# Order of ScalarE's copies at the first FFN pair, and the last FFN chunk in two passes over the token columns

## The chip, the core and the metric

The kernel runs on one core of a Trainium2 chip. The core has a matrix engine (TensorE, PE in the profile, its weight loads listed as PEld), VectorE (DVE), ScalarE (ACT), GpSimd (POOL) and SyncE (SP), which issues most of the DMAs. Each engine works through its own queue in order and waits for the others by semaphores. Matrix products are summed in PSUM; all else lies in SBUF. The metric is the device time of one execution in microseconds (us); lower is better.

## What is computed

One step of a one-layer hybrid encoder on 512 prompt tokens, 16 meta tokens and 32 sample tokens: RMSNorm, one input projection, a gated linear attention branch and a softmax branch, their gated sum, an output projection, then the feed-forward part and a last RMSNorm:

```python
m = jax.nn.sigmoid(ga) * ya + jax.nn.sigmoid(gb) * yb
h = h + jnp.einsum('btd,de->bte', m, w_out)
u = jnp.einsum('btd,df->btf', _rmsnorm(h, norm_ffn), w_up)
h = h + jnp.einsum('btf,fd->btd', jnp.square(jax.nn.relu(u)), w_down)
...
y_prompt = _rmsnorm(h_p[:, N_META:], norm_final)
y_sample = _rmsnorm(h_s, norm_final)
```

The model width is 1024 (8 blocks of 128), the FFN width 4096. All is float32.

## The kernel before

Activations lie transposed: 128 features on the partitions, the tokens along the free dimension. From the output projection on there are 544 token columns (32 of the sample, 512 of the prompt). To be exact in the fast float32 mode of the matrix engine, each operand is split into a rounded part (`split_hi`, a copy on ScalarE, line 121) and a rest (`split_lo`, a subtraction on VectorE, line 124), and each product is three matmuls: hi by hi, lo weight by hi, hi weight by lo. All matmuls have one helper and so one line (118); tiles tell them apart.

**Order.** From the output projection on, TensorE, ScalarE and VectorE run in exactly the order in which the program emits their instructions. SP's DMAs wait for the buffer that they write.

**Output projection (`ps_wo`).** Eight steps n over the output blocks d in the order 0, 4, 1, 5, 2, 6, 3, 7. A step splits the weights of the next block (`wh`, `wl`), runs 48 matmuls, adds the result to the residual (line 1237) and calls `operands(d)`. That function makes the FFN's right-hand operands: for d < 4 one pair of half-width tiles; for d of 4 or more, sums and differences (lines 1214 to 1221) and the splits called BN, B21 and BT4 (tiles `hh`, `hl`). Steps 1, 3, 5 and 7 have d of 4 or more.

**FFN, upward (`up_pair(g)`, 16 pairs).** Each pair makes four column groups of u by a seven-product scheme on halves (272 tokens wide): products of 12 matmuls into two PSUM tiles X and V that are copied out and then added to further, and Y. In order: X from a11, V from s1, X from s2, V from s4, X from s3, Y from a12, X from a22. X's product from s2 may start only when `fa` has taken the first X out of PSUM (ScalarE, line 1335); V's product from s4 only when `fb` has taken V (line 1341). Then comes relu squared (lines 1362, 1369) and its splits (`uh`, `ul`); those of the second half are put into the list `tail` and emitted in the next pair, ahead of `fa`'s copy. The weights of pair g+1 are prepared meanwhile by the generator `pair_prep` in seven steps: four DMAs (tile `wr`, three buffers), the sums s31 and s24 on VectorE (lines 287, 290, 294), the splits of a11, s1, then s2 and s4 together, then s3 and a12, then a22. Before pair 0 all of that is emitted ahead of the first copy of X.

**FFN, downward (`down(c, d)`).** Eight chunks c of 512 rows, eight output blocks d; 24 matmuls each, 288 and 256 columns wide in two PSUM tiles. Chunk c runs between the products of the pairs of chunk c+1; its weights come from `down_prep` (a DMA into `dr`, then the splits `dh`, `dl`, two buffers each). The first chunk's first weights are split in pair 2, just ahead of `down(0, 0)`. Results are summed into `acc`; the last chunk's are scaled by `r2`, added to the residual (lines 1423, 1425), and finished.

**The end.** The last chunk has no pairs beside it. `final_part(g, tiles)` transposes a group of blocks back to token rows (groups of 4, 3 and 1 blocks; line 1280, tile `ps_fin`), sums squares on ScalarE (line 1282) and multiplies by the weight on VectorE (line 1283, `ytok`). Tile 0 is the sample (32 tokens), tiles 1 to 4 are 128 prompt tokens each. `final_norm` makes the reciprocal root (lines 1296 to 1298, 399 to 401), scales (600 columns on VectorE, line 1305, 424 on ScalarE, line 1306) and starts the output DMAs (line 1308). Group 0 runs inside d = 4, group 1 inside d = 7, group 2 after it: tiles 0 to 2 after the first 288 columns, tiles 3 and 4 after the other 256.

Of the kernel before, what the change touches and what calls it, by code (L numbers as in the profile page):

```python
# [8 lines left out]
F32 = mybir.dt.float32  # L9
# [38 lines left out]
def tile_hybrid_step(  # L48
# [256 lines left out]
    def down_prep(c, d):  # L305

        if c == NCH - 1:
            raw = wpool.tile([P, K4, P], F32, tag="raw", name=f"dr{c}_{d}", bufs=3)
        else:
            raw = blk([K4, P], F32, f"dr{c}_{d}", "v")  # L310
        SP.dma_start(raw, w_down[0, 512 * c: 512 * c + 512, P * d: P * d + P].rearrange("(k p) n -> p k n", p=P))
        yield
        hi, lo = [pairw["L"].tile([P, K4, P], F32R, tag="d" + x, name=f"d{x}{c}_{d}", bufs=2) for x in "hl"]
        split_hi(hi, raw)
        split_lo(lo, raw, hi)
        downs[c, d] = (hi, lo)
        yield
# [875 lines left out]
    def operands(d, mid=None):  # L1193
        j, g = d % 4, gffn[:, d: d + 1]
        H_, L_ = hH[j], hL[j]

        def hi(i, src):
            split_hi(H_[:, i: i + src.shape[1], :], src)

        def lo(i, src):  # L1200
            split_lo(L_[:, i: i + src.shape[1], :], src, H_[:, i: i + src.shape[1], :])


        if d < 4:
            ba, bb = bts[0] = half_pair(f"ba{j}"), half_pair(f"bb{j}")
            ACT.activation(ba[:, 0, :], hs[d][:, 0:HT], AF.Copy, scale=g)
            ACT.activation(bb[:, 1, :], hs[d][:, HT:], AF.Copy, scale=g)
            DVE.tensor_tensor(ba[:, 1, :], ba[:, 0, :], bb[:, 1, :], ALU.subtract)
            hi(B11, ba)
            lo(B11, ba)  # L1210
            return
        ba, bb = bts[0]
        b2 = half_pair(f"b2{j}")
        ACT.activation(b2, halves(hs[d]), AF.Copy, scale=g)
        DVE.scalar_tensor_tensor(bb[:, 0, :], ba[:, 1, :], -1.0, b2[:, 1, :], ALU.mult, ALU.subtract)
        DVE.tensor_tensor(bb[:, 1, :], b2[:, 1, :], bb[:, 1, :], ALU.subtract)
        if mid:
            mid()
        hi(BN, bb)
        hi(B21, b2)  # L1220
        DVE.scalar_tensor_tensor(ba[:, 0, :], bb[:, 0, :], -1.0, b2[:, 0, :], ALU.mult, ALU.subtract)
        lo(BN, bb)
        hi(BT4, ba[:, 0:1, :])
        lo(B21, b2)
        lo(BT4, ba[:, 0:1, :])

    bts = [None]
    for n, d in enumerate(WO_ORDER):
# [12 lines left out]
        hs[d] = xr
        operands(d, (lambda: go(prep, 1)) if n == KD - 1 else None)
# [41 lines left out]

    s3b = cpool.tile([P, NTT], F32, name="s3b")

    def final_early():

        DVE.tensor_tensor(s3b, s3[:, :, 0], s3[:, :, 1], ALU.add)
        DVE.tensor_scalar(s3b, s3b, 1.0 / D, EPS, ALU.mult, ALU.add)  # L1290

    def final_norm(t0, t1):
        w = t1 - t0
# [22 lines left out]
                mm(ps[:, :HT], w[w_][:, j, :], x_[j][:, b, :], start and n == 0, n == 11)  # L1316
                n += 1

    tail = []

    def up_pair(g):

        nonlocal prep
        drain(prep) if g == 0 else None
        W = pairs.pop(g)
        uh = upool.tile([P, 4, HT], F32R, tag="uh", name=f"uh{g}")
        ul = upool.tile([P, 4, HT], F32R, tag="ul", name=f"ul{g}")
        us[g] = (uh, ul)
        fa, fb = half_pair(f"fa{g}"), half_pair(f"fb{g}")
        X, V = psm(f"ps_x{g}"), psm(f"ps_v{g}")  # L1330
        xv, vv = X[:, :HT], V[:, :HT]
        product(X, W["a11"], B11, True)
        while tail:
            tail.pop(0)()
        ACT.activation(fa[:, 0, :], xv, AF.Copy)  # L1335
        go(prep, 1)
        prep = pair_prep(g + 1) if g < 15 else iter(())
        go(prep, 1)
        yield
        product(V, W["s1"], BM, True)  # L1340
        ACT.activation(fb[:, 1, :], vv, AF.Copy)
        yield
        product(X, W["s2"], BN, False)
        ACT.activation(fa[:, 1, :], xv, AF.Copy)
        go(prep, 1)
        yield
        product(V, W["s4"], B22, False)
        go(prep, 1)
        DVE.tensor_tensor(fa[:, 1, :], vv, fa[:, 1, :], ALU.add)
        yield  # L1350
        product(X, W["s3"], BT3, False)
        x3 = fpool.tile([P, HT], F32, tag="x3", name=f"x3_{g}", bufs=1)
        go(prep, 1)
        ACT.activation(x3, xv, AF.Copy)
        DVE.tensor_tensor(fb[:, 1, :], x3, fb[:, 1, :], ALU.add)
        yield
        Y = psm(f"ps_y{g}")
        yv = Y[:, :HT]
        product(Y, W["a12"], B21, True)
        go(prep, 1)  # L1360
        DVE.tensor_tensor(fa[:, 0, :], yv, fa[:, 0, :], ALU.add)
        DVE.scalar_tensor_tensor(fa, fa, 0.0, fa, ALU.max, ALU.mult)
        yield
        product(X, W["a22"], BT4, False)
        split_hi(uh[:, 0:2, :], fa)
        go(prep, 1)
        split_lo(ul[:, 0:2, :], fa, uh[:, 0:2, :])
        ACT.activation(fb[:, 0, :], xv, AF.Copy)
        DVE.scalar_tensor_tensor(fb, fb, 0.0, fb, ALU.min, ALU.mult)

        def rest():
            split_hi(uh[:, 2:4, :], fb)
            split_lo(ul[:, 2:4, :], fb, uh[:, 2:4, :])

        tail.append(rest)
        yield
# [8 lines left out]
            dpreps[i] = down_prep(*dn[i])  # L1385
            go(dpreps[i], 1)

    def down(i, mid=None):
        c, d = dn[i]
        if i + 1 < len(dn):  # L1390
            go(dpreps[i + 1], 1)
        dstart(i + 2)
        wh, wl = downs.pop((c, d))
        psf = (psa, pss)[d % 2]
        pd = [psf(f"ps_dn{c}_{d}_{ci}") for ci in range(2)]
        for ci, ks in (((0, (0, 1)), (1, (0, 1)), (0, (2, 3)), (1, (2, 3))) if d == 0 else
                       ((0, range(4)), (1, range(4)))):
            a, b = OC[ci]
            if mid and ci == 1:
                mid()  # L1400
            for k in ks:
                uh, ul = [u[:, 2 * (k % 2): 2 * (k % 2) + 2, :].rearrange("p s t -> p (s t)")
                          for u in us[2 * c + k // 2]]
                for m, (w_, x_) in enumerate(((wh, uh), (wl, uh), (wh, ul))):
                    mm(pd[ci][:, : b - a], w_[:, k, :], x_[:, a:b], k == 0 and m == 0, k == 3 and m == 2)
        for ci in range(2):
            evac_down(c, d, ci, pd[ci])

    def evac_down(c, d, ci, ps):
        a, b = OC[ci]  # L1410
        w = b - a
        if c == 0:
            if ci == 0:
                acc[d] = blk([TM], F32, f"acc{d}", "v")
            ACT.activation(acc[d][:, a:b], ps[:, :w], AF.Copy)
        elif c < NCH - 1:
            DVE.tensor_tensor(acc[d][:, a:b], ps[:, :w], acc[d][:, a:b], ALU.add)  # L1417
            if c == NCH - 2:
                DVE.tensor_tensor(acc[d][:, a:b], acc[d][:, a:b], r2[:, a:b], ALU.mult)
                DVE.tensor_tensor(hs[d][:, a:b], acc[d][:, a:b], hs[d][:, a:b], ALU.add)  # L1420
        else:
            dt_ = fpool.tile([P, TM], F32, tag="dt", name=f"dt{c}_{d}_{ci}", bufs=2)
            DVE.tensor_tensor(dt_[:, :w], ps[:, :w], r2[:, a:b], ALU.mult)
            if d < 7 or ci == 0:
                DVE.tensor_tensor(hs[d][:, a:b], hs[d][:, a:b], dt_[:, :w], ALU.add)
            if d == 7:
                tiles = ((0, 1, 2), (3, 4))[ci]
                final_part(2, tiles, (dt_, a) if ci else None)
                final_norm(tiles[0], tiles[-1] + 1)

    def square(d):

        if d == 0:
# [17 lines left out]
    for c in range(NCH):  # L1451
        for jj in range(2):
            slots = up_pair(2 * c + jj)
            for n, _ in enumerate(slots):
                if c > 0 and n in (1, 3, 5, 6):
                    d = 4 * jj + (1, 3, 5, 6).index(n)
                    if d == 0 and c == 1:
                        go(dpreps[0], 1)
                    down(8 * (c - 1) + d)
                    if c == 1:  # L1460
                        square(d)
# [44 lines left out]
```

## Time and profile before

| | us |
|---|---|
| median of three runs | 850.74 (850.53 to 851.29) |
| profiled execution | 847.04 |
| span of its profile (first to last instruction) | 845.2 |

The profiled execution has 1.84 us around its span and lies 3.70 us under the median of the runs. In the page's first part TensorE is busy 96% of the span, VectorE 69%, ScalarE 43%. In the second part (40 slices of 21.1 us) TensorE's digit is 9 in nearly all slices; it falls to 7 and 6 in the slices that begin at 444 and 465 us and to 3 in the last one, from 824 us. A row of a timeline has the start, the time, engine, line, operation, output and inputs, shape and count, and in brackets the idle time before it with what ended it. A merged row of several instructions gives the time from the first start to the last end; matmuls overlap, so the pitch of a row of n is its time less that of one, over n - 1.

### The profile page before, as it was taken

Reading aid. Unit: us, or ns where it says so; the run is one execution under the profiler, and the core shown is the slowest. Engines: PE = TensorE matmul, PEld = TensorE weight load, DVE = VectorE, ACT = ScalarE, POOL = GpSimd, SP = SyncE. Lnnn points to the kernel's source line nnn. Section 1 sums busy time; section 2 is a strip of 40 time slices with the busy share of each in tenths; the row PEclk is TensorE's granted clock in tenths of the full one; section 3 lists DMA queues with packets and bytes.
Section 4 is the critical chain, followed back from the end, with each engine's and each line's share of the span. In section 5 each row is a group of like instructions: output and inputs, shape, how many; then the busy total and the mean of one; then the engine's idle time right before and its main releaser. Section 6 shows DMA issues by size and latency. Waiting matters only on the chain.

```text
span 845.2 us, 15168 instructions
## 1 busy us (share of the span) xinstructions
PE 808.9 (96%) x6087; PEld 776.3 (92%) x6087; DVE 583.7 (69%) x1139; ACT 367.1 (43%) x723; POOL 122.9 (15%) x131
## 2 busy tenths in 40 slices
PE   8999999999999999999997699999999999999993
PEld 7877889898999999999997699999999999999993
DVE  6865348798758564466677856787777777779884
ACT  6760454555445633232445465433433443344233
POOL 4315111121122393025000000000000000000000
PEclk9997999999999999999999999999999999999997
DMA  8612214421521133233321322333333333322112
GB/s 243 165 51 82 50 43 103 122 77 50 134 77 50 51 85 91 85 91 111 97 82 50 106 69 77 88 88 101 100 100 101 88 100 101 91 80 81 50 50 106
DMA packets 133813, 75.38 MB, mean 89 GB/s; under 512 B 15056, under 2 KB 129024, under 8 KB 133744
## 3 DMA queue, kind: packets, MB, share of 16 engines
q1 hardware_dynamic: 132704, 72.27, 30.4%
q0 software_dynamic: 1024, 2.14, 1.1%
q8 instruction: 48, 0.79, 0.4%
q14 instruction: 21, 0.17, 0.1%
q10 hardware_dynamic: 16, 0.00, 0.0%
HBM read 69.57 MB, written 4.83 MB: 88 GB/s over the span
## 4 chain that ended last, share of the span: by engine, by line
PE 77%; DVE 9%; ACT 5%; POOL 3%; issue 2%; DMA 2%; SPq 0%; ACTq 0%; DVEq 0%; POOLq 0%
PE ps_dn L118 23%; PE ps_x L118 10%; PE ps_gb L118 5%; PE ps_ga L118 5%; PE ps_v L118 5%; PE ps_wo L118 4%; PE ps_fv L118 3%; PE ps_ya L118 3%; PE ps_yb L118 2%; PE ps_fk L118 2%; PE ps_y L118 2%; PE ps_fq L118 2%; PE ps_gv L118 1%; PE ps_pv L118 1%; PE ps_s L118 1%
## 5 line engine op out<-in xcount | busy, mean ns | idle before, releaser
L118 PE MATMUL ps_dn<-uh,dh 128*128 128x288 f32 (+1 forms) x512 | 148.0, 289 | 3.9 <-ACT dh L121 3.9
L118 PE MATMUL ps_dn<-uh,dl 128*128 128x288 f32 (+1 forms) x512 | 148.9, 291 | 0.3 <-DVE dl L124 0.3
L118 PE MATMUL ps_dn<-ul,dh 128*128 128x288 f32 (+1 forms) x512 | 148.4, 290 | 0.0
L118 PEld LDWEIGHTS ps_dn<-uh,dh 128*128 128x128 f32 x512 | 97.2, 190 | 4.1 <-ACT dh L121 4.1
L118 PEld LDWEIGHTS ps_dn<-uh,dl 128*128 128x128 f32 x512 | 97.0, 190 | 0.5 <-DVE dl L124 0.5
L118 PEld LDWEIGHTS ps_dn<-ul,dh 128*128 128x128 f32 x512 | 97.0, 189 | 0.1
L121 ACT ACTIVATE wh<-wr 128x1024 fp32r<-128x1024 f32 x46 | 48.5, 1055 | 91.9 <-PE ps_yb L118 24.0
L124 DVE TENSOR_TENSOR wl<-wr,wh 128x1024 fp32r<-128x1024 f32 x46 | 69.6, 1513 | 17.2 <-ACT wh L121 16.5
L243 POOL TENSOR_TENSOR wr<-wr,gmix 128x1024 f32<-128x1024 f32 x30 | 58.2, 1942 | 145.2 <-DMA wr<-in_w_in_dram 56.3
L1417 DVE TENSOR_TENSOR acc<-ps_dn,acc 128x288 f32<-128x288 f32 x96 | 41.1, 438 | 30.6 <-PE ps_dn L118 30.6
L1261 POOL DMA_DIRECT2D gfin<-in_norm_final_dram x1 | 0.6, 607 | 396.1 <-DVE acc L1417 396.1
L124 DVE TENSOR_TENSOR dl<-dr,dh 128x512 fp32r<-128x512 f32 x64 | 43.8, 686 | 9.4 <-ACT dh L121 9.3
L121 ACT ACTIVATE dh<-dr 128x512 fp32r<-128x512 f32 x64 | 39.9, 624 | 13.9 <-PE ps_dn L118 13.9
L118 PE MATMUL ps_x<-hh,whi 128*128 128x272 f32 x128 | 37.9, 296 | 7.2 <-ACT fa L1335 7.2
L118 PE MATMUL ps_x<-hh,wlo 128*128 128x272 f32 x128 | 37.5, 293 | 0.0
L118 PE MATMUL ps_x<-hl,whi 128*128 128x272 f32 x128 | 37.5, 293 | 0.0
L118 PE MATMUL ps_v<-hh,whi 128*128 128x272 f32 x128 | 37.1, 290 | 0.0
L118 PE MATMUL ps_v<-hl,whi 128*128 128x272 f32 x128 | 37.1, 290 | 0.0
L118 PE MATMUL ps_v<-hh,wlo 128*128 128x272 f32 x128 | 37.0, 289 | 0.0
L124 DVE TENSOR_TENSOR wlo<-s,whi 128x512 fp32r<-128x512 f32 (+1 forms) x32 | 30.6, 955 | 6.4 <-ACT whi L121 6.4
L896 ACT ACTIVATE sb<-sb,m 128x144 f32<-128x144 f32 (+3 forms) x32 | 18.3, 573 | 34.0 <-DVE m L891 34.0
L118 PEld LDWEIGHTS ps_x<-hh,whi 128*128 128x128 f32 x128 | 24.7, 193 | 7.7 <-ACT fa L1335 7.7
(473 smaller groups left out, 2284.8 us busy)
## 6 DMA issues: line engine op xcount, KB each, us to landing
dr<-in_w_down_dram SPq DMA_DIRECT2D x64, 256.0 KB, 3.1
wr<-in_w_up_dram SPq DMA_DIRECT2D x64, 256.0 KB, 3.1
wr<-in_w_in_dram SPq DMA_DIRECT2D x30, 512.0 KB, 3.9
wr<-in_w_out_dram SPq DMA_DIRECT2D x8, 512.0 KB, 4.1
cb<-cPd SPq DMA_DIRECT2D x8, 264.0 KB, 4.3
x_t<-in_x_prompt_dram SPq DMA_DIRECT2D x4, 512.0 KB, 5.4
gvraw<-in_w_in_dram SPq DMA_DIRECT2D x4, 512.0 KB, 8.3
fvraw<-in_w_in_dram SPq DMA_DIRECT2D x4, 512.0 KB, 3.7
```

What stands on the lines that cost most here:

```text
L118: return TE.matmul(out, lhsT, rhs, start=start, stop=stop, skip_group_check=True)
L121: ACT.activation(out, in_, AF.Copy)
L124: (eng or DVE).tensor_tensor(out, in_, hi.bitcast(F32), ALU.subtract)
L243: POOL.tensor_tensor(raw, raw, gmix.unsqueeze(2).to_broadcast([P, KD, P]), ALU.mult)
L896: exps.append(ACT.activation(sb, sb, AF.Exp, bias=m, scale=-1.0, accum_out=rs).ins)
L1261: POOL.dma_start(late["gfin"], norm_final.partition_broadcast(P))
L1417: DVE.tensor_tensor(acc[d][:, a:b], ps[:, :w], acc[d][:, a:b], ALU.add)
```

## The change

1. **operands(d), d of 4 or more.** The order of emission becomes BN hi, BN lo, B21 hi, B21 lo, the difference of line 1221, BT4 hi, BT4 lo. For the last block (d = 7) all after BN goes into `tail`.
2. **up_pair.** `fa`'s copy of X comes ahead of the list `tail` and of the rest of `pair_prep`. For pair 0 the splits of s3, a12 and a22 now come after that copy (and after the deferred part of `operands(7)`), but ahead of `fb`'s copy of V. After X's product from a22 the preparation step (s3, a12) comes ahead of the split of `fa` into `uh`.
3. **First down weights.** The split of the first `dr` moves from pair 2 into pair 1, after V's product from s4.
4. **Last chunk.** `down` serves it no more. Pass one runs all eight d over columns 0 to 416 (tiles 0 to 3), pass two over columns 416 to 544 (tile 4), 12 matmuls each; the weights of d of 2 and more stay in buffers of their own. The final parts of tiles 0 to 3 run inside pass one (group 0, at d = 4) and pass two (groups 1 and 2, at d = 1 and 2; `final_norm` at d = 3), those of tile 4 at d = 6 and 7 and behind.

```diff
@@ down_prep @@
-        hi, lo = [pairw["L"].tile([P, K4, P], F32R, tag="d" + x, name=f"d{x}{c}_{d}", bufs=2) for x in "hl"]
+        hi, lo = [(late["yp"].tile([P, K4, P], F32R, tag="l" + x, name=f"d{x}{c}_{d}", bufs=KD - 2) if c == NCH - 1 and d > 1 else
+                   pairw["L"].tile([P, K4, P], F32R, tag="d" + x, name=f"d{x}{c}_{d}", bufs=2)) for x in "hl"]
@@ operands @@
         hi(BN, bb)
-        hi(B21, b2)
-        DVE.scalar_tensor_tensor(ba[:, 0, :], bb[:, 0, :], -1.0, b2[:, 0, :], ALU.mult, ALU.subtract)
         lo(BN, bb)
-        hi(BT4, ba[:, 0:1, :])
-        lo(B21, b2)
-        lo(BT4, ba[:, 0:1, :])
+
+        def rest():
+            hi(B21, b2)
+            lo(B21, b2)
+            DVE.scalar_tensor_tensor(ba[:, 0, :], bb[:, 0, :], -1.0, b2[:, 0, :], ALU.mult, ALU.subtract)
+            hi(BT4, ba[:, 0:1, :])
+            lo(BT4, ba[:, 0:1, :])
+
+        if mid:
+            tail.append(rest)
+        else:
+            rest()
@@ up_pair @@
-        drain(prep) if g == 0 else None
...
         product(X, W["a11"], B11, True)
+        ACT.activation(fa[:, 0, :], xv, AF.Copy)
         while tail:
             tail.pop(0)()
-        ACT.activation(fa[:, 0, :], xv, AF.Copy)
-        go(prep, 1)
+        drain(prep)
...
         product(X, W["a22"], BT4, False)
+        go(prep, 1)
         split_hi(uh[:, 0:2, :], fa)
-        go(prep, 1)
         split_lo(ul[:, 0:2, :], fa, uh[:, 0:2, :])
@@ main loop @@
+                if c == 0 and jj == 1 and n == 3:
+                    go(dpreps[0], 1)
...
-                    if d == 0 and c == 1:
-                        go(dpreps[0], 1)
@@ the last chunk, in place of down(8 * (NCH - 1) + d, ...) @@
+    CUT2 = OT[4][0]
+
+    def last(d, a, b, psf):
+        wh, wl = downs[c, d]
+        ps = psf(f"ps_dn{c}_{d}_{a}")
+        for k in range(4):
+            uh, ul = [u[:, 2 * (k % 2): 2 * (k % 2) + 2, :].rearrange("p s t -> p (s t)") for u in us[2 * c + k // 2]]
+            for m, (w_, x_) in enumerate(((wh, uh), (wl, uh), (wh, ul))):
+                mm(ps[:, : b - a], w_[:, k, :], x_[:, a:b], k == 0 and m == 0, k == 3 and m == 2)
+        return ps
...
     for d in range(KD):
-        down(8 * (NCH - 1) + d, {4: lambda: final_part(0, range(NTT)), 7: last_but_one}.get(d))
+        if d + 1 < KD:
+            go(dpreps[8 * c + d + 1], 1)
+        dstart(8 * c + d + 2)
+        ps = last(d, 0, CUT2, (psa, pss)[d % 2])
+        if d == 4:
+            final_part(0, range(4))
+        rest = last_evac(d, 0, CUT2, ps)
+    for d in range(KD):
+        ps = last(d, CUT2, TM, (psa, pss)[d % 2])
+        if d == 1:
+            final_part(1, range(4))
+        if d == 2:
+            final_part(2, range(4), rest)
+            final_early(0, 4)
+        if d == 6:
+            final_part(0, [4])
+        if d == 7:
+            final_part(1, [4])
+            final_early(4, 5)
+        rest2 = last_evac(d, CUT2, TM, ps)
+        if d == 3:
+            final_norm(0, 4)
+    final_part(2, [4], rest2)
+    final_norm(4, 5)
```

## Rows read from the trace of the kernel before

**Rows 1.** TensorE's waits, 425 to 500 us: in total, times, longest.

```profile
PE ps_x L118 <- ACT fa L1335: 7.2, 2, 4.3
PE ps_dn L118 <- ACT dh L121: 3.9, 1, 3.9
```

**Rows 2.** Busy time by stretch; near the end PEclk, the granted share of TensorE's clock.

```profile
452.50:455.70 3.20, 3.12 (x14) 3.12 (x15) 1.00 (x2) 0.31 (x2) 0.00 (x0) 0.50 0.49 140
...
520.00:780.00 260.00, 259.45 (x2057) 258.94 (x2056) 195.91 (x334) 104.22 (x201) 0.00 (x0) 1.00 0.32 92
...
76.00:80.00 4.00, 4.00 (x22) 3.12 (x19) 0.28 (x2) 0.00 (x0) 0.00 (x0) 0.50 0.50 135
```

**Rows 3.** The chain that ended last, 430 to 520 us: start, us, what.

```profile
452.93 2.92 DMA wr<-in_w_up_dram
...
483.22 4.62 PE ps_dn L118 x23
```

**Rows 4.** VectorE's timeline, 425 to 490 us.

```profile
435.25 0.44 DVE L1221 SCALAR_TENSOR_TENSOR ba<-bb,b 128x272 f32<-128x272 f32 x1
436.06 0.72 DVE L124 TENSOR_TENSOR hl<-bb,hh 128x544 fp32r<-128x544 f32 x1 [0.37 <-ACT hh L121]
436.70 0.72 DVE L124 TENSOR_TENSOR hl<-b,hh 128x544 fp32r<-128x544 f32 x1
...
437.88 1.23 DVE L124 TENSOR_TENSOR wl<-wr,wh 128x1024 fp32r<-128x1024 f32 x1
...
464.19 0.69 DVE L124 TENSOR_TENSOR s3l<-s,s3h 128x512 fp32r<-128x512 f32 x1 [1.25 <-ACT s3h L121]
...
480.86 0.72 DVE L124 TENSOR_TENSOR ul<-fb,uh 128x544 fp32r<-128x544 f32 x1 [0.72 <-ACT uh L121]
```

**Rows 5.** ScalarE's timeline, 425 to 486 us.

```profile
436.48 0.42 ACT L121 ACTIVATE hh<-ba 128x272 fp32r<-128x272 f32 x1
436.80 1.05 ACT L121 ACTIVATE wh<-wr 128x1024 fp32r<-128x1024 f32 x1
...
452.13 0.40 ACT L1335 ACTIVATE fa<-ps_x 128x272 f32<-128x272 f32 x1
...
462.98 0.66 ACT L121 ACTIVATE uh<-fa 128x544 fp32r<-128x544 f32 x1 [2.40 <-DVE fa L1362]
...
481.81 1.15 ACT L121 ACTIVATE dh<-dr 128x512 fp32r<-128x512 f32 x2
```

**Rows 6.** TensorE's timeline in the last step of the output projection.

```profile
440.04 1.09 PE L118 MATMUL ps_wo<-mh,wl 128*128 128x288 f32 x7
```

**Rows 7.** TensorE's timeline: 512 columns, 128 columns, transposes, the last chunk's ends.

```profile
59.56 2.01 PE L118 MATMUL ps_gv<-gvl,xh 128*128 128x512 f32 x8
...
172.09 0.22 PE L118 MATMUL ps_s<-kh,pq 128*128 128x128 f32 x1
172.16 0.27 PE L118 MATMUL ps_s<-kl,pq 128*128 128x128 f32 x1
...
800.70 0.30 PE L118 MATMUL ps_dn<-uh,dh 128*128 128x288 f32 x1
...
814.55 1.91 PE L1280 MATMUL ps_fin<-ident,xres 128*32 128x128 f32 x16
...
829.65 0.28 PE L118 MATMUL ps_dn<-ul,dh 128*128 128x256 f32 x1
```

**Rows 8.** VectorE's timeline in the last chunk, first final part.

```profile
815.89 3.07 DVE L1283 TENSOR_TENSOR ytok<-ps_fin,gfin 32x512 f32<-32x512 f32 x5 [1.25 <-ACT fj L1282]
```

**Rows 9.** ScalarE's timeline, the last scaling of the output.

```profile
838.76 1.19 ACT L1306 ACTIVATE ytok<-ytok,r3r 128x424 f32<-128x424 f32 x2 [0.62 <-DVE r3r L401]
```

**Rows 10.** The chain that ended last, 780 to 846 us: start, us, what.

```profile
826.33 0.34 PE ps_fin L1280 x3
...
827.36 2.42 DVE ytok L1283 x5
...
835.48 1.67 PE ps_fin L118 x6
```

More of the change, by code (lines that the diff above doesn't have):

```diff
@@ L1219, in operands @@
         hi(BN, bb)
-        hi(B21, b2)
-        DVE.scalar_tensor_tensor(ba[:, 0, :], bb[:, 0, :], -1.0, b2[:, 0, :], ALU.mult, ALU.subtract)
         lo(BN, bb)
-        hi(BT4, ba[:, 0:1, :])
-        lo(B21, b2)
-        lo(BT4, ba[:, 0:1, :])
+        def rest():
[8 more added lines that the diff above has]
+            rest()
     bts = [None]
+    tail = []
     for n, d in enumerate(WO_ORDER):
@@ L1285, in tile_hybrid_step, with final_early @@
     s3b = cpool.tile([P, NTT], F32, name="s3b")
-    def final_early():
-        DVE.tensor_tensor(s3b, s3[:, :, 0], s3[:, :, 1], ALU.add)
-        DVE.tensor_scalar(s3b, s3b, 1.0 / D, EPS, ALU.mult, ALU.add)
+    def final_early(t0, t1):
+        DVE.tensor_tensor(s3b[:, t0:t1], s3[:, t0:t1, 0], s3[:, t0:t1, 1], ALU.add)
+        DVE.tensor_scalar(s3b[:, t0:t1], s3b[:, t0:t1], 1.0 / D, EPS, ALU.mult, ALU.add)
     def final_norm(t0, t1):
@@ L1317, in product @@
                 n += 1
-    tail = []
     def up_pair(g):
         nonlocal prep
-        drain(prep) if g == 0 else None
         W = pairs.pop(g)
@@ L1386, in dstart, with down @@
             go(dpreps[i], 1)
-    def down(i, mid=None):
+    def down(i):
         c, d = dn[i]
@@ L1398, in down @@
             a, b = OC[ci]
-            if mid and ci == 1:
-                mid()
             for k in ks:
@@ L1420, in evac_down @@
                 DVE.tensor_tensor(hs[d][:, a:b], acc[d][:, a:b], hs[d][:, a:b], ALU.add)
[L1421 to L1429, printed above, removed]
     def square(d):
@@ L1466, in tile_hybrid_step, with last_evac @@
     alloc_ytok()
-    def last_but_one():
-        final_part(1, range(NTT))
-        final_early()
-    for d in range(KD):
-        down(8 * (NCH - 1) + d, {4: lambda: final_part(0, range(NTT)), 7: last_but_one}.get(d))
+    c = NCH - 1
+    CUT2 = OT[4][0]
[7 more added lines that the diff above has]
+        return ps
+    def last_evac(d, a, b, ps):
+        dt_ = fpool.tile([P, TM], F32, tag="dt", name=f"dt{c}_{d}_{a}", bufs=2)
+        DVE.tensor_tensor(dt_[:, : b - a], ps[:, : b - a], r2[:, a:b], ALU.mult)
+        if d < KD - 1:
+            DVE.tensor_tensor(hs[d][:, a:b], hs[d][:, a:b], dt_[:, : b - a], ALU.add)
+        return dt_, a
+    for d in range(KD):
+        if d + 1 < KD:
[22 more added lines that the diff above has]
+    final_norm(4, 5)
 _INS = ['x_prompt', 'x_sample', 'cache_fox_k', 'cache_fox_v', 'cache_fox_logf', 'state_gla', 'meta_tokens',
```

## The prediction

> **What bounds the kernel now.** I read the page's slices first: TensorE is full nearly everywhere, so the only time to be had is where its digit falls, at the first FFN pairs and behind the last matmul. Then TensorE's waits around the first pairs: 7.2 us in two waits for ScalarE's copy of X, the longer one 4.3, and 3.9 for `dh`, the first split of the down weights [rows 1]. The stretches show what a wait costs besides: after the 4.3 us TensorE runs 3.2 us at a granted clock of 0.50, the lower level, 1.2 GHz; and in the 260 us from 520 it is busy 259.45, so what is gained or lost before the chunks stays so [rows 2]. The chain of waits shows who feeds these waits: VectorE's splits, then a DMA at 452.93 that needs a buffer freed by VectorE's split of a12, 2.92 us to landing, and at the end 23 matmuls of the first down block in 4.62 us [rows 3], where a pitch of 0.13 would make 3.0. So around the first pairs VectorE's queue and that DMA set the pace, not ScalarE alone.
>
> **Operand order: a loss of 1.1 us on TensorE.** In steps 1, 3 and 5 of the output projection the difference of line 1221 (435.25, 0.44) now stands behind both rests instead of ahead of them. BN lo starts at 436.06 as before, B21 lo 0.64 later, so the difference runs at 437.34 and ends at 437.78 [rows 4]. BT4 hi can only follow it, and the next weights' `wh` comes 0.32 behind BT4 hi: 438.12 in place of 436.80 [rows 5]. `wl` (437.88, [rows 4]) follows the end of `wh` and moves by the same 1.3, to an end of 440.4. TensorE takes `wl` at 440.04 and `wh` seven matmuls of pitch 0.133 earlier, at 439.1 [rows 6]: `wh` is just in time, `wl` 0.4 late. Three steps, 1.1 us. When VectorE comes to the last step it is 2.0 late (1.3, and two of the three TensorE waits).
>
> **First pair: about nothing.** `fa`'s copy of X ran at 452.13, behind six other copies [rows 5]. Now it stands behind BN hi alone, which is 2.0 late: I get 450.9, and X's product from s2 begins at 451.3, 1.2 sooner. But `fb`'s copy of V has not moved ahead: queued before it are B21, BT4, s3, a12 and a22 hi (2.5 us), and BT4 now waits some 1.6 us for VectorE's difference behind the B21 rest. `fb` runs at about 455.1, so V's product from s4 waits 2.5 us and begins at 455.6, where it begins now. Behind `fb` on ScalarE are all copies of pair 0; none is needed earlier. On VectorE the split of a12 moves by 2.0 and 0.6 of waiting for BT4 hi, so the DMA of 452.93 goes out at 455.6 and pair 1's sums begin at 458.7, 2.65 late [rows 3].
>
> **Preparation ahead of the split of fa: 1.3 us back per pair.** ScalarE idles 2.40 us before `uh` [rows 5]; s3 and a12 hi (1.05) fit in there, and VectorE's 1.25 us wait for s3 hi goes [rows 4]. This takes the 2.65 to 1.3 at the end of pair 0. In pair 1 VectorE gets the new `dl` (0.6) and again 1.3 back, and some short waits shrink, so its last split, `ul` of the second half, ends where it did, at 481.6 [rows 4].
>
> **The first down weights: 5.2 us gained.** Before, `dh` ran at 481.81, behind the late second-half copy `uh` [rows 5], and all 24 matmuls of the first down block stood behind it, to 487.84 [rows 3]. After, they begin where V ends, at about 478.6. The first 15 need nothing late; the rest wait for `uh` and `ul` of pair 1 (481.6), then 7 matmuls of 0.12 and the drain follow: end 482.6, a gain of 5.2. Bounds: with TensorE at half clock there (24 matmuls of 0.23, the 4.62 over 23 being partly at the full clock) the end is 484.6, a gain of 3.2; 5.6 if VectorE gets through sooner. I take 5.2: in this walk TensorE has no wait in the 9 us before. What is late next: nothing that I find, as the next weights' DMAs wait for pair 2's a22 buffer, as now, and should land about 1 us ahead of need.
>
> **Last chunk: a loss on TensorE.** The same 192 weight loads now serve 416 and 128 columns in place of 288 and 256. The pitch at 512 columns is (2.01 - 0.39)/7 = 0.23, at 288 it is 0.133 [rows 6, 7]; 416 lies between, 0.187. For 128 columns the trace has few back-to-back pairs: the second matmul of one starts 0.07 after the first, but ends 0.12 after it (172.43 against 172.31): it started and had to wait for its own weights. Transposes of 128 columns, each with a new stationary block, come at (1.91 - 0.28, the length of one)/15 = 0.11 [rows 7]. So a matmul of 128 columns is bound by its weight load, between 0.107 and 0.13; I take 0.114. The Trainium skill (TensorE: Matmul & The Clock Gate, "Back-to-back issue gap") gives about 81 ns for a stream of 128-column matmuls with weight loads, an estimate of 3.2 us less for the 96; the same page's "LDWEIGHTS" section gives 107 ns for 128 weight columns, and the ends in this trace agree with the latter.
>
> Sum on TensorE: 96 x 0.187 = 17.9; 96 x 0.114 = 10.9; 32 transposes of 0.11, 3.5; eight full-precision matmuls of two passes, 1.8. New waits: 0.4 at the start for VectorE, and 1.4 at d = 6, since `dl` of d = 6 now stands behind four `ytok` products of 0.6 [rows 8] and the evacuation of d = 4. Together 35.9. Before: 800.70 to 829.77, 29.1 [rows 7]. Loss 6.8.
>
> **The end: a gain of 4.4 us.** Before, 10.2 us lie between the last matmul and the last scaling's end (838.76 + 1.19 = 839.95) [rows 9]. After, only tile 4 is left. Its group 1: the chain from 826.33 to the end of the five `ytok` (829.78), 3.45, less four of the five (4 x 0.485), 1.5 [rows 10]; the two small sums behind and the evacuations of d = 6 and 7, ahead and behind, make it an estimated 2.7. Its group 2: from 835.48 to 839.95 it is 4.5 now; one tile instead of two takes 1.0 from the 1.67 of matmuls and 0.54 from the scaling [rows 9, 10], leaving 3.0 to 3.1. 5.8 in all, 4.4 less. The output DMA after it stays. Cover: `final_norm` of tiles 0 to 3 and their DMAs hide under pass two; VectorE has about 10 us of work in its 14.
>
> **Sum.** The span of 845.2 less 5.2, plus 6.8, less 4.4: 842.6. With the 1.84 around it 844.4, and with the 3.70 by which the profiled execution lies under the median: 848.1 us, 0.3% faster. A difference of about 0.2% (1.7 us) is what a measurement of this kernel can tell from none.
>
> **Rivals.** *The narrow pass is cheap.* If the start difference of 0.07 is the true pitch [rows 7], 96 matmuls save 4.2 us; VectorE, whose evacuations of d = 4 to 6 then stand behind `final_norm`, gives back 1.5: 845.4. For it speaks that starts are recorded and ends modelled; against it the transposes at 0.11. The skill's 81 ns would lie between, at about 846. *The clock falls in pass two* (ends slower). TensorE is then counted busy, but streams less than half of the time; between 76 and 80 us it was busy 4.00 of 4 us beside narrow products at a granted clock of 0.50 [rows 2]. Against it: the transposes at 814.55 keep their pitch. At half clock the pitch goes from 0.114 at most to the double (in the first down block it went from 0.13 to 4.62/23 = 0.20, partly at the full clock [rows 3]): about 0.09 each, 8.7 us for all 96, 856.8. It ends slower than before once some 47 of the 96 run so. *The first pairs give back.* V's copy behind the deferred work, several gaps of 1 to 2.5 us and with them the lower clock into the first down block (3.2 in place of 5.2), and a DMA that lands 1.4 us later through VectorE's queue: a gain of 1.8 instead of 5.2, 851.5, no change. It decides if `ul` of pair 1 ends after 483.
>
> **Chances.** As worked out 0.62 (own range 846.8 to 850.0, from 0.107 to 0.13 and the bounds of the down block); cheap narrow pass 0.15; first pairs give back 0.14; clock falls 0.09. Two thirds of the first case lie under 849.0, with the second that makes faster 0.59; within 0.2% 0.28 (the rest of the first, most of the third); slower 0.13. The range of 845.2 to 852.0 leaves out the falling clock and little else.
>
> **What would show it.** TensorE's waits: X for `fa` shrinks to about 1.5 us, a new one of about 2.5 appears for `fb` in pair 0, none is left for `dh`; `wl` delays steps 3, 5 and 7 by 0.4. The first down block ends 5 us earlier. In pass two 12 matmuls take 1.37 us; a `dl` wait of about 1.4 stands in pass one; about 6 us lie behind the last product in place of 10. Wrong would be: 12 in 0.85, a clock under 1.0 in pass two, or the down block at 485 or later.

## The result, and the profile after

The changed kernel takes 846.38 us (median of 4 runs, 845.29 to 847.36) beside 850.63 for the kernel before in the same comparison: ratio 0.9949, 95% interval 0.9931 to 0.9966, so 4.25 us or 0.5% faster. A second comparison, with 12 runs against 29, gave 845.58 beside 850.36 and a ratio of 0.9942 (0.9912 to 0.9971). The forecast was 848.1. Most runs of the kernel before lie near 846 us or near 851 (in the second comparison 11 of 29 are under 847).

The profiled execution of after took 846.18 us, its span 844.5, close to its median. The one of before lay 3.70 under its own. So the two spans differ by 0.7 us only, and they are not to be compared as they stand: the projection, `ps_wo`, begins at 395.7 us before and at 397.6 after, behind code that is the same in both. I therefore read every trace from the start of the projection, in stages: the projection (first to last matmul on `ps_wo`); the pairs (from there to the first matmul behind the first down block); the middle (to the last matmul on `ps_x`); the chunk (to the last matmul on `ps_dn`); the end (to the start of the last scaling on ScalarE); the rest (to the end of the span).

The page of after, TensorE's line and its two lines of slices (tenths busy, tenths of the clock granted):

```profile
PE 815.0 (97%) x6096; PEld 779.2 (92%) x6096; DVE 583.4 (69%) x1140; ACT 367.1 (43%) x723; POOL 122.9 (15%) x131
...
PE   8999999999999999999997899999999999999995
...
PEclk9997999999999999999999999999999999999998
```

The five longest of TensorE's waits of after from 400 us on (total, times, longest), which answer [rows 1]:

```profile
PE ps_v L118 <- ACT fb L1347: 3.2, 2, 2.3
PE ps_x L118 <- ACT fa L1339: 1.7, 2, 1.5
PE ps_fin L118 <- DVE dt L1477: 1.5, 1, 1.5
PE ps_dn L118 <- DVE dl L124: 1.2, 1, 1.2
PE ps_v L118 <- DVE fa L1367: 0.7, 1, 0.7
```

The two long waits for `fa` (7.2 us) and the one for `dh` (3.9) are gone; in their place stand several short ones, for `fb` above all. Stretches of after (busy time of PE, PEld, DVE, ACT, POOL, then PEclk) that answer [rows 2]:

```profile
452.50:454.50 2.00, 0.68 (x4) 0.60 (x5) 1.85 (x3) 1.79 (x4) 0.00 (x0) 1.00 0.00 0
454.50:456.50 2.00, 1.24 (x10) 1.01 (x9) 1.50 (x4) 0.81 (x2) 0.00 (x0) 1.00 0.00 0
456.50:458.50 2.00, 0.49 (x4) 0.49 (x5) 1.92 (x4) 2.00 (x6) 0.00 (x0) 1.00 0.00 0
...
482.50:486.50 4.00, 3.77 (x28) 3.33 (x27) 3.24 (x6) 3.25 (x7) 0.00 (x0) 1.00 0.81 228
820.00:834.00 14.00, 14.00 (x127) 13.71 (x125) 9.41 (x32) 7.44 (x27) 0.00 (x0) 1.00 0.17 57
```

TensorE does little from 452.5 to 458.5, but in bits, and its clock stays at 2.4 GHz, also under the first down block (482.5 to 486.5) and in the narrow pass (820 to 834).

The chain that ended last, of after (start, us, what), which answers [rows 3, 10]:

```profile
429.60 1.24 DVE wl L124
430.84 0.04 issue
430.88 5.35 PE ps_wo L118 x41
...
457.99 3.00 DMA wr<-in_w_up_dram
...
815.50 7.24 PE ps_dn L118 x47
...
837.27 0.50 PE ps_fin L118 x2
...
839.40 0.65 ACT ytok L1315
```

Already in the projection the chain runs through VectorE's `wl`; the DMA that [rows 3] had at 452.93 is still on it.

All stages, worked out from the first and last starts of those groups (us, rounded; the profiled execution of each run; the experiments follow, of which e5 to e8 ran once each, on another chip, where e8 shows the stages of before to be the same):

| kernel | begins | projection | pairs | middle | chunk | end | rest | from the projection on |
|---|---|---|---|---|---|---|---|---|
| before | 395.7 | 49.3 | 42.7 | 309.9 | 32.1 | 9.7 | 5.8 | 449.4 |
| after | 397.6 | 50.9 | 36.5 | 309.9 | 39.3 | 5.2 | 5.1 | 446.9 |
| e1 chunk only | 395.4 | 49.2 | 42.7 | 309.9 | 39.3 | 5.2 | 5.1 | 451.4 |
| e2 pairs only | 397.7 | 50.9 | 36.5 | 309.9 | 32.1 | 9.7 | 5.8 | 444.9 |
| e3 prep and dr | 396.4 | 49.3 | 35.3 | 309.9 | 32.1 | 9.7 | 5.8 | 442.1 |
| e4 dr only | 394.5 | 49.2 | 40.3 | 309.9 | 32.1 | 9.7 | 5.9 | 447.0 |
| e5 old order, cut 288 | 399.3 | 49.3 | 35.6 | 309.9 | 35.1 | 7.9 | 5.8 | 443.6 |
| e6 prep, dr, fa; pass of 32 | 398.4 | 49.2 | 34.9 | 309.9 | 43.4 | 4.9 | 4.4 | 446.8 |
| e7 prep only; ytok 2 + 2 | 398.3 | 49.3 | 40.9 | 310.0 | 39.0 | 5.5 | 5.1 | 449.7 |
| e8 before, again | 396.2 | 49.2 | 42.8 | 309.9 | 32.1 | 9.7 | 5.8 | 449.5 |
| e9 prep, dr, fa | 393.4 | 49.2 | 34.9 | 309.9 | 32.1 | 9.7 | 5.8 | 441.6 |
| e10 after, again | 396.9 | 51.0 | 36.4 | 309.9 | 39.3 | 5.5 | 5.1 | 447.1 |
| e11 before, third | 398.3 | 49.2 | 45.1 | 309.9 | 32.1 | 9.6 | 5.8 | 451.7 |
| e12 dr only, again | 398.8 | 49.2 | 39.2 | 309.9 | 32.1 | 9.7 | 5.9 | 445.9 |

Apart from the pairs, a stage of the same code repeats within 0.3 us, so there one trace settles what a timing of this kernel can't. The pairs of before took 42.7, 42.8 and 45.1. From the projection on, after is 2.5 us shorter than the first trace of before: 1.7 lost in the projection, 6.2 gained in the pairs, 7.2 lost in the chunk, 4.5 + 0.8 gained behind it. The forecast's terms for these, 5.2 and 4.4 less 6.8, make 2.8.

### The profile page after: what moved, and what is told of

Read it like the earlier page. It is cut to its first block, busy times and chain, and to the rows that moved or that the text cites. A ratio compares the mean times of both kernels' runs of the same rounds, so it can differ in the third digit from the quotient of the medians.

```text
span 844.5 us, 15178 instructions
## 1 busy us (share of the span) xinstructions
PE 815.0 (97%) x6096; PEld 779.2 (92%) x6096; DVE 583.4 (69%) x1140; ACT 367.1 (43%) x723; POOL 122.9 (15%) x131
## 4 chain that ended last, share of the span: by engine, by line
PE 72%; DVE 14%; ACT 4%; DMA 3%; POOL 3%; issue 3%; SPq 1%; DVEq 0%; POOLq 0%; ACTq 0%
PE ps_dn L118 22%; PE ps_x L118 10%; PE ps_gb L118 5%; PE ps_v L118 5%; PE ps_ga L118 4%; PE ps_fv L118 3%; PE ps_ya L118 3%; PE ps_yb L118 2%; PE ps_y L118 2%; PE ps_wo L118 2%; PE ps_gv L118 2%; DVE wl L124 2%; PE ps_fk L118 1%; PE ps_gr L118 1%; PE ps_gq L118 1%
## 5 line engine op out<-in xcount | busy, mean ns | idle before, releaser
L118 PE MATMUL ps_dn<-uh,dl 128*128 128x288 f32 (+3 forms) x512 | 149.8, 292 | 1.2 <-DVE dl L124 1.2
L118 PE MATMUL ps_dn<-ul,dh 128*128 128x288 f32 (+3 forms) x512 | 149.3, 292 | 0.2 <-DVE ul L124 0.2
L118 PE MATMUL ps_dn<-uh,dh 128*128 128x288 f32 (+3 forms) x512 | 149.0, 291 | 0.0
L121 ACT ACTIVATE whi<-s 128x512 fp32r<-128x512 f32 (+1 forms) x32 | 26.8, 839 | 9.3 <-DVE s L287 5.6
```

The costliest lines, as they stand in the source:

```text
L118: return TE.matmul(out, lhsT, rhs, start=start, stop=stop, skip_group_check=True)
L121: ACT.activation(out, in_, AF.Copy)
```

## The experiments

Theory (that of the forecast): the first pairs are paced by VectorE's queue and the DMA behind it; the move of the first down split (with s3 and a12 ahead) is the gain, fa's copy is worth nothing, the operand order costs, and the last chunk is a net loss, since a narrow matmul costs its weight load. Rivals: fa's early copy is what gains; the chunk pays for itself; the surplus of the measured gain over the sum lies in one of the parts.

**e1, the chunk alone.** The kernel before with after's `down_prep`, `final_early`, `last`, `last_evac` and final loops.

```diff
-        down(8 * (NCH - 1) + d, {4: lambda: final_part(0, range(NTT)), 7: last_but_one}.get(d))
+        ps = last(d, 0, CUT2, (psa, pss)[d % 2])
...
+        ps = last(d, CUT2, TM, (psa, pss)[d % 2])
```

> The kernel before with the two passes of the last chunk alone. By the terms of the forecast: 6.8 us more on TensorE, 4.4 less behind the last matmul, so 2.4 us slower than before (ratio 1.0028); 12 narrow matmuls in 1.37 us or less, about 6 us behind the last product. Rival, from the measured gain of 4.25 us for the whole change where the forecast's terms made 2.8: the surplus lies in the chunk, which then costs about 1.0 (1.0012).

Measured: ratio 1.0022 (0.9998 to 1.0045), 1.9 us slower; the stages too say 1.9. The chunk loses. This is between the two expectations and nearer to the forecast's 2.4. The times alone rule out neither of them, nor quite that nothing is lost; the stages decide.

**e2, the pairs alone.** Everything but the hunks of e1.

> The whole change but for the last chunk, which stays as before. By the terms of the forecast: the first down block ends 5.2 us earlier and nothing else moves, so 5.2 us faster than before (0.9939). Rival: the surplus of 1.45 us over the forecast's sum lies in the first pairs, 6.7 us faster (0.9921).

Measured: 0.9927 (0.9897 to 0.9958), 6.2 us faster; by the stages 4.5. The interval holds 5.2 as well as 6.7. If the timed gain has a surplus over the sum, it is here, with the pairs, and no stage of this trace shows it. e11 takes this up.

**e3, only the two moves.** Operand order, the rest of d = 7 and fa's place as before.

```diff
         product(X, W["a22"], BT4, False)
+        go(prep, 1)
         split_hi(uh[:, 0:2, :], fa)
-        go(prep, 1)
...
+                if c == 0 and jj == 1 and n == 3:
+                    go(dpreps[0], 1)
                 if c > 0 and n in (1, 3, 5, 6):
                     d = 4 * jj + (1, 3, 5, 6).index(n)
-                    if d == 0 and c == 1:
-                        go(dpreps[0], 1)
```

> The kernel before with two moves alone: the split of s3 and a12 ahead of the first-half split of fa, and the first split of the down weights in pair 1. Operand order, deferred rest and the place of fa's copy stay as before. By the forecast's theory the new operand order costs 1.1 us on TensorE and makes VectorE 2.0 late, and fa's earlier copy gains nothing, so this kernel is 1.5 to 2.4 us faster than the one with all changes of the pairs: 6.7 to 7.6 us faster than before (0.9911 to 0.9921). Rival: fa's earlier copy is worth its 2 to 3 us of wait, and without it the gain is 3 us or less (0.9965).

Measured: 0.9884 (0.9851 to 0.9918), 9.9 us faster; the stages say 7.4, inside the forecast's 6.7 to 7.6. TensorE's waits of e3 between the projection and the first down block:

```profile
PE ps_x L118 <- ACT fa L1335: 6.2, 2, 4.3
```

The wait for `fa` of 4.3 us is all there, and the pairs are 1.2 us shorter than with the whole change, which cut it to 1.5. So this wait costs next to nothing (e6 puts it at 0.4 us); what matters comes later. The rival falls.

**e4 and e12, the down split alone**, the second hunk of e3.

> The kernel before with the first split of the down weights in pair 1 alone. By the forecast's theory its 3.9 us wait and the half clock behind it go, and VectorE's last split of pair 1 comes 0.6 later through the new split: 4.3 to 4.9 us faster (0.9942 to 0.9949), nearly the whole gain of the first pairs. Rival: what sets the end of pair 1 is VectorE's queue, in which the new split now stands too, so that the wait only moves to the last split of pair 1: 2 us or less (0.9976).

> The first down split in pair 1 alone, again. Its first trace had 447.0 us from the start of the projection, 2.5 less than before, with a stretch of half clock of some 6 us in pair 1 that the other kernels don't have; its runs were 7.2 less. If that stretch belongs to the program, it is there again (40.3 us from the projection to the end of the first down block); if it was a chance of that execution, 37 us, which is what the walk through the queues gives without it.

Measured: 0.9915 (0.9881 to 0.9949) and, with 12 runs, 0.9947 (0.9921 to 0.9972); by the stages 2.4 and 3.5 us in place of the 4.3 to 4.9. The wait for `dh` is gone in both, as expected. What was not expected is in the stretches. Of e4:

```profile
465.70:467.70 2.00, 1.08 (x5) 1.08 (x6) 1.31 (x2) 1.67 (x4) 0.00 (x0) 0.50 0.83 245
467.70:469.70 2.00, 2.00 (x10) 2.00 (x10) 1.94 (x3) 0.00 (x0) 0.00 (x0) 0.50 0.27 74
469.70:471.70 2.00, 2.00 (x11) 2.00 (x10) 0.69 (x1) 1.95 (x4) 0.00 (x0) 0.50 0.64 191
```

And of e12:

```profile
470.00:472.00 2.00, 1.14 (x9) 1.14 (x10) 1.36 (x3) 1.61 (x4) 0.00 (x0) 1.00 0.83 248
472.00:474.00 2.00, 2.00 (x13) 2.00 (x12) 1.97 (x4) 1.15 (x3) 0.00 (x0) 0.57 0.26 76
474.00:476.00 2.00, 2.00 (x11) 2.00 (x11) 0.94 (x3) 0.81 (x2) 0.00 (x0) 0.58 0.63 186
```

Pair 1 begins, after a second wait for `fa` of some 3 us, at the lower clock, for about 7 us in the one execution (465.6 to 472.4) and under 4 in the other (472.3 to 475.7): 10 or 11 matmuls in 2 us instead of the 18 that e4 has from 472.4 on. The same program, then, has this stretch both times, but not of the same length; its length goes with the difference of 1.2 us between the two traces, and with part of what was missing. The 39.2 us of e12 lie between its two expectations.

**e7, s3 and a12 ahead alone**, the first hunk of e3; and, in the chunk, `ytok` of the first group in two portions (`if d in (4, 5): final_part(0, range(2 * d - 8, 2 * d - 6))`).

> Two stages. First: the kernel before with s3 and a12 ahead of the first-half split alone, the first down split left where it was. If VectorE's queue is the chain, this alone brings pair 1's last split 2.6 us forward, and the first down block ends 2.6 to 3.5 us earlier, 39.2 to 40.1 us behind the projection (before 42.7; the move of the down split alone gave 40.3, both together 35.3); rival, it only fills idle time of ScalarE: 42 or more. Second: the two passes cut at 416 as in the change, with tiles 0 and 1 of the first column group taken at d = 4 and tiles 2 and 3 at d = 5 instead of all four at d = 4. If dl of d = 6 waited for four ytok products, its wait of 1.2 us goes and the chunk takes 38.1 us to its last product instead of 39.3; rival, dl of d = 7 waits as long: 39.3.

Measured: pairs 40.9, a gain of 1.8 where 2.6 to 3.5 was expected. The wait for `dh` fell from 3.9 to 2.5, but TensorE ran at half clock longer, from 455.6 to beyond 459.6 us:

```profile
455.60:457.60 2.00, 2.00 (x10) 2.00 (x10) 0.51 (x1) 0.00 (x0) 0.00 (x0) 0.50 0.35 103
457.60:459.60 2.00, 2.00 (x10) 2.00 (x10) 0.95 (x1) 0.92 (x2) 0.00 (x0) 0.50 1.03 292
...
485.60:487.60 2.00, 2.00 (x10) 2.00 (x10) 0.86 (x2) 0.13 (x1) 0.00 (x0) 0.50 0.90 217
```

and the first down block (485.6) still did; whether that is all that is missing is not shown. Each move alone gives 1.8 and 2.4 to 3.5, both together 7.4: the two clear the way to the block only together, and with the last long wait goes the half clock that came behind it (in e3 the granted clock is 1.00 from 457 us on). In the chunk the wait for `dl` at d = 6, 1.25 us in after, is gone as expected, but one of 0.68 has come at d = 7 (at 821.06): the rival, half as large. The chunk took 39.0 us, not 38.1, and chunk, end and rest together stayed at 49.6: a miss. The longer end, 5.5, is not its doing, as e10 has it with after's own code.

**e5, old operand order; the chunk cut at column 288.** In the pairs, for d = 4 to 6 the order B21 hi, difference, BN lo, BT4 hi, B21 lo, BT4 lo of before; in the chunk `C1, C2 = (0, 288), (288, 544)` and tiles 0 to 2, then 3 and 4.

> Two stages that don't touch each other. First: the whole change of the pairs, but with the operand order of before for the token halves of d = 4 to 6 (fa's copy ahead, the deferred rest and both moves stay). If the new order is what makes TensorE wait for wl, the projection takes 49.3 us again instead of 50.9, and from it to the end of the first down block it is 35.3 to 35.6 (36.5 with the order); rival, the order pays for itself in the pairs: over 36.5. Second: the last chunk cut at column 288 instead of 416, tiles 3 and 4 in pass two. If a narrow matmul costs its weight load, 288 and 256 columns cost what they did before: 32.2 to 32.9 us from the start of the chunk to its last product (before 32.1, cut at 416 39.3), and with two tiles left behind it 11.5 to 12.5 us to the end of the span (before 15.5, cut at 416 10.3). Rival, a second pass costs by itself, through its repeated loads and waits: 35 or more.

Measured: projection 49.3, pairs 35.6. The new order costs 1.7 us in the projection and 0.9 in the pairs, with no return. What e5 keeps of the change, the deferred rest of d = 7, seems to cost as well: e6 and e9, which defer nothing, have pairs of 34.9, 0.7 less. The chunk, though, took 35.1, which is the rival's number, and 13.8 us followed it instead of 11.5 to 12.5. TensorE's waits in it and, the first of them, behind it:

```profile
PE ps_fin L118 <- DVE dt L1482: 1.8, 1, 1.8
PE ps_dn L118 <- DVE dl L124: 1.3, 1, 1.3
PE ps_fin L1294 <- DVE xres L1484: 0.8, 1, 0.8
PE ps_dn L118 <- DVE ul L124: 0.6, 1, 0.6
```

A matmul of 288 or 256 columns costs what it did; the waits for `dl` and `ul`, 1.9 us, and the final work of tiles 0 to 2, which now lies ahead of the last product, are what is left to make the 3.0 us. That they make all of it is argued, not shown. In all 48.9 from the chunk's start to the end of the span, beside 47.6 undivided, 49.6 cut at 416 and, in e6, 52.7 with 32 columns apart: none of the divisions tried pays.

**e6, fa's copy with both moves; a last pass of 32 columns.** `ACT.activation(fa[:, 0, :], xv, AF.Copy)` ahead of the drained preparation (in later pairs ahead of `tail`), nothing deferred; `C1, C2 = (32, 544), (0, 32)`.

> Two stages. First: the kernel with the two moves (s3 and a12 ahead of the split, first down split in pair 1), and besides fa's copy of pair 0 ahead of the drained preparation, with nothing deferred and the operand order of before. If VectorE's queue and the DMA behind it set the pace, TensorE's wait for fa shrinks by some 2 us and another wait takes its place: 35.3 us from the projection to the end of the first down block, as without it; rival, X's wait counts: 33.5 or less. Second: the last chunk with 512 columns in pass one and the 32 columns of tile 0 in pass two. If a narrow matmul is bound by its weight load, 12 of them take 1.33 us as at 128 columns (0.11 each); rival, they are bound by their columns: 0.5 us or less. Pass one takes 96 x 0.23 = 22.1 us, as 512 columns do elsewhere.

Measured: pairs 34.9, 0.4 less than e3. `fa`'s wait shrank to 2.7 at most and 0.9 for `fb` took its place; so fa's copy is worth some 0.4 us, not its wait. Pass one, 22.1 us by its matmuls, took 24.9 with transposes and a wait of 0.9 for `dl` in it. TensorE in the pass of 32 columns, and a stretch of it:

```profile
829.24 0.26 PE L118 MATMUL ps_dn<-ul,dh 128*128 128x32 f32 x1
829.35 0.26 PE L118 MATMUL ps_dn<-uh,dh 128*128 128x32 f32 x1
829.46 0.26 PE L118 MATMUL ps_dn<-uh,dl 128*128 128x32 f32 x1
...
835.22 0.37 PE L118 MATMUL ps_dn<-ul,dh 128*128 128x32 f32 x1
835.43 0.37 PE L118 MATMUL ps_dn<-uh,dh 128*128 128x32 f32 x1
...
830.00:835.00 5.00, 5.00 (x40) 4.91 (x40) 3.32 (x12) 3.06 (x7) 0.00 (x0) 0.83 0.58 224
```

Starts lie 0.11 apart, as with 128 columns: a quarter of the columns costs the same, and the weight loads (PEld) fill 4.91 of 5 us, so it is the weight load that binds. And here the clock does fall, to 0.50 from some 833 us on (0.83 is the mean of the stretch), with starts 0.21 apart: the price of the forecast's second rival, 0.10 each where 0.09 was put down.

**e9, the version that the stages point to**: e6's pairs with the chunk of before.

> The version that the stages point to: fa's copy of pair 0 ahead of the drained preparation, s3 and a12 ahead of the first-half split, the first down split in pair 1; operand order, rest and last chunk as before. From the stages of the traces: projection 49.2, to the end of the first down block 34.9, from there to the last chunk 309.9, chunk 32.1, behind it 15.5, in sum 441.6 from the start of the projection where before takes 449.5: 7.9 us faster (0.9907). Rival, the last chunk or the middle gives something back: over 443.5 from the start of the projection.

Measured: 0.9892 (0.9852 to 0.9932), 9.2 us faster, and 441.6 from the projection on, as expected to the tenth. By the stages it is 7.8 us faster than before and 5.3 faster than after. It and e3 can't be told apart by time.

**e8, e10, e11, the two kernels again.**

> The kernel before, unchanged, for a second trace. The runs of before lie in two groups, near 845 to 847 and near 850 to 852 us; the first trace is of the lower one. If this one is of the upper group, it shows where the 4 to 5 us lie: ahead of the projection, in code that no kernel here changes (the projection begins 4 us later, the stages behind it have the same lengths), or in the first pairs, whose half clock then lasts longer (over 45 us from the projection to the end of the first down block).

> The changed kernel, unchanged, with more runs. From the projection on its first trace is 2.6 us shorter than before (446.9 against 449.5), while its runs were 4.25 shorter. If the stages behind the projection's start are all there is, the ratio is 0.997 (2.6 us); if the part ahead of it, the same code in all kernels, is shorter too, 0.995 again. The stages repeat within 0.2 us.

> The kernel before against itself, as the measure of what the comparison can tell: ratio 1.000. If a copy of the same program has a level of its own, 0.996 to 0.998 or 1.002 to 1.004. Its trace should have 449.5 us from the start of the projection, whatever the span.

Measured: e8 has the stages of the first trace (one run, 847.62 us). e10 gave 0.9942 and the stages of after. e11 against before gave 1.0009 (0.9979 to 1.0039), so a copy has no level of its own that this can tell; but its trace, of an execution with a span of 849.9, is 4.8 us longer than the first of before: 2.5 of them ahead of the projection, 2.4 in the pairs. Stretches of e11:

```profile
470.00:474.00 4.00, 3.57 (x21) 3.57 (x22) 3.76 (x5) 2.62 (x7) 0.00 (x0) 0.73 0.60 172
474.00:480.00 6.00, 6.00 (x45) 6.00 (x45) 3.98 (x8) 1.34 (x2) 0.00 (x0) 0.89 0.12 36
...
487.00:489.00 2.00, 1.88 (x8) 1.62 (x8) 2.00 (x3) 0.12 (x1) 0.00 (x0) 0.50 0.58 163
489.00:491.00 2.00, 2.00 (x11) 2.00 (x11) 0.76 (x2) 0.00 (x0) 0.00 (x0) 0.50 0.81 212
```

Its waits are those of [rows 1] (7.4 and 3.9 us). What is longer is the half clock behind them: in pair 1, where the first trace had none, and under nearly the whole first down block. Against this, e10, also with a stretch at half clock (458 to 460, behind the wait for `fb`):

```profile
456.00:458.00 2.00, 0.63 (x3) 0.63 (x4) 1.90 (x3) 2.00 (x5) 0.00 (x0) 0.84 0.00 0
458.00:460.00 2.00, 2.00 (x10) 2.00 (x10) 0.00 (x0) 0.12 (x1) 0.00 (x0) 0.50 0.68 204
```

has pairs of 36.4 us, against 36.5 without it: there VectorE and the DMA end last, and a slow TensorE hides under them.

Ahead of the projection the clock differs as well, in code that all kernels share. The same 40 us in before, e3 and e9:

```profile
60.00:100.00 40.00, 37.91 (x260) 32.27 (x259) 19.90 (x51) 7.49 (x14) 15.73 (x17) 0.87 0.31 81
...
60.00:100.00 40.00, 38.19 (x267) 32.18 (x266) 21.03 (x53) 7.72 (x15) 16.19 (x17) 0.91 0.32 81
...
60.00:100.00 40.00, 37.90 (x278) 32.16 (x279) 22.50 (x56) 9.87 (x20) 17.09 (x18) 1.00 0.31 81
```

From the first matmul on `ps_gq` to the first on `ps_fk` it takes 56.4 to 56.5 us in the nine traces with about 10 us at half clock there, 54.7 in the four with about 7, and 52.0 in e9, which has none. e11 and the first trace of before are alike in this; of e11's 2.5 us, 2.2 stand already at the first matmul on `ps_gq` (64.25 against 62.00), and e11 ran at half clock from 7.6 to 14.4 us, before did not. How much of the 2.2 that makes is not shown.

Not tried: V's copy for `fb` ahead of the deferred work as well. `fb` is written into a buffer that the deferred splits still read, so the order can't be had without another buffer.

## Why the prediction was right, and where it was off

The sign, the range and the mechanism held; the gain was 4.25 us where 2.6 was forecast. In part that is luck: the projection with the pairs, and the chunk, came out 1.1 us worse than their terms, and the end, with a term that was left out, 0.9 better, so that the stages still make 2.5 of 2.8. The sum has a slip, too: 845.2 less 5.2, plus 6.8, less 4.4 is 842.4, not 842.6, so the forecast by its own terms is 847.9. Its chances for faster add up to 0.56, not 0.59, and 29 matmuls at half clock would use up the 2.6 us, its 47 only with some 0.2% on top. By its own steps, in which the stages of after are set against the first trace of before, from the start of the projection on (1.9 us later in after):

**Operand order: right, undersized.** 1.7 us instead of 1.1. In step 3 of the projection, ScalarE of after:

```profile
415.60 0.43 ACT L121 ACTIVATE hh<-ba 128x272 fp32r<-128x272 f32 x1 [1.23 <-DVE ba L1226]
415.94 1.05 ACT L121 ACTIVATE wh<-wr 128x1024 fp32r<-128x1024 f32 x1
```

and TensorE:

```profile
416.78 0.28 PE L118 MATMUL ps_wo<-ml,wh 128*128 128x256 f32 x1
417.04 1.19 PE L118 MATMUL ps_wo<-mh,wh 128*128 128x288 f32 x7
418.30 1.20 PE L118 MATMUL ps_wo<-mh,wl 128*128 128x288 f32 x7
```

BT4 hi waits 1.23 us for the difference, as forecast, and `wh` follows it. `wh` was forecast just in time; it is 0.14 late (417.04 against 416.78 + 0.12), and `wl` another 0.33 (418.30 against 417.04 + 7 x 0.133). Three steps of 0.47 are 1.4 of the 1.7. No line of the waits lists these: each gap is too short for it. The chain shows them.

**First pair: right.** X's product from s2 begins at 453.82, in the time of before 451.9 (forecast 451.3); V's from s4 at 458.01, or 456.1 (455.6), behind the forecast wait for `fb`, 2.27 us for 2.5; the DMA goes at 457.99, or 456.1 (455.6). All three are late by about the 0.6 that the operand order cost more. e6 puts fa's copy at 0.4 us, the forecast's "about nothing".

**Preparation ahead, and the first down weights: right together, wrong in their shares.** `ul` of pair 1 begins at 483.29, ending in the time of before at 482.1 (481.6), under the 483 from which the third rival decides; the block ends 4.5 us earlier, counted with the projection's loss, for 5.2. Of the 0.7 between them 0.6 is the projection's. What the forecast had as 5.2 for the down split and 1.3 a pair for the order is not a sum: alone they gave 2.4 to 3.5 and 1.8, together 7.4 (e3, e4, e7, e12).

**Last chunk: right.** From its first matmul (798.07) to the end of the last (834.50) 36.4 us, for 35.9; before 29.2; loss 7.2 for 6.8. TensorE of after where the narrow pass begins:

```profile
819.95 0.22 PE L118 MATMUL ps_dn<-uh,dh 128*128 128x128 f32 x1
820.01 0.27 PE L118 MATMUL ps_dn<-uh,dl 128*128 128x128 f32 x1
820.12 0.27 PE L118 MATMUL ps_dn<-ul,dh 128*128 128x128 f32 x1
820.23 0.28 PE L118 MATMUL ps_dn<-uh,dh 128*128 128x128 f32 x1
```

The first pair starts 0.06 apart, where [rows 7] had 0.07, and from then on it is 0.11; 12 take 1.34 us for 1.37. So the start difference of a lone pair was no pitch, and the first rival falls. The trace of before had a sign of it, the matmul behind the pair of [rows 7], 0.11 after the second:

```profile
172.27 0.23 PE L118 MATMUL ps_s<-mask_b,ident_b 128*128 128x128 bf16 x1
```

The formula of the Trainium skill (TensorE: Matmul & The Clock Gate, "LDWEIGHTS") makes 107 ns for 128 weight columns, an estimate that agrees with the 0.11; the 81 ns of that page's "Back-to-back issue gap" no stream of matmuls with 128 weight columns here reached. The wait for `dl` at d = 6 was 1.25 for 1.4. The second rival, too, falls for this kernel: the granted clock is 1.00 in pass two. e6 shows it at 32 columns.

**The end: right, and one term left out.** From the last matmul's end to the last scaling's end (840.05) 5.55 us for 5.8. But "the output DMA after it stays" was wrong: from there to the end of the span it is 4.45 instead of 5.25. With two tiles left, in e5, it is 5.24 again (842.9 less 837.66): the last of two transfers ends later than one alone, and SyncE waits 2.9 us for it in before and in e5, 2.2 in after. That is 0.8 us.

**The step that failed is the last line of the sum:** the 3.70 us by which the profiled execution of before lies under its median, added to after as it was. After's lies 0.2 under its own. The first trace of before is of the lower of its two groups of runs. e11, of the upper, shows 2.4 of the 4.8 us as half clock behind the long waits of the first pairs, which the change takes away; a gain counted on the first trace, 2.5 us, is counted on that one 4.8, and 4.25 and 4.8 were measured. The other 2.5 lie ahead of the projection, whose start varies from 393.4 to 399.3 us over the 14 traces with the same code ahead of it. That the groups go with the clock every run shows: in the second comparison the mean granted clock is 0.982 to 0.986 in the 11 runs of before under 847 us and 0.974 to 0.980 in the 18 others, all above 848. From the first trace's 0.984 to the median's 0.980 it is some 6 us more at half clock, which would cost a busy TensorE some 3 us of the 3.70, an estimate. Where in those runs they lie only e11 shows. In line with it, e1, which keeps the pairs of before, lost as much in time as in stages, while every kernel with other pairs and more than one run gained 1.0 to 4.8 us more in time than in stages. Why the runs of e4 were that much shorter than its trace lets expect (7.2 against 2.4, in e12 4.5 against 3.5), stays open.

## What to carry to other kernels

Read a change of 0.5% in stages from a common point, not in spans: outside the pairs stages repeat within a few tenths while the span varies by 5 us. Look at the granted clock first where the same code takes two lengths. Ask of each wait what ends last behind it, since 4.3 us of waiting cost next to nothing here while 3.9 in front of a block of matmuls cost more than themselves through the clock; and two moves on one chain may be worth little alone and all together. Before a split into a narrow pass, count weight loads, not columns: it bought 5.3 us at the end for 7.2 of TensorE, and the best versions here (e3 and e9, 9 to 10 us faster in their runs, 7.4 and 7.8 by the stages) leave the last chunk and the operand order alone.

## What the runs showed of the hardware

A matmul with 128 weight columns of its own takes 0.11 us from start to start with 128 and with 32 columns alike. The granted clock fell under a dense stream of 32-column matmuls, with TensorE's record busy throughout, and did not with 128 columns. Behind the same waits in the same program, the stretch at half clock was of different length from one execution to the next: about 7 us or under 4 in pair 1 with the down split alone, none or some 3.5 us there in before. Ahead of the projection the same code took 52.0, 54.7 or 56.5 us, with none, about 7 or about 10 us of it at half clock. And the end of the program depends on how many output transfers are still behind one another: 0.8 us for the second.
